# A two-layer hybrid block on one core: side transfers cut in pieces and set between weight loads, first groups paired, new layer's operand in four chains

## The chip, the cores and the metric

One core of a Trainium2 chip runs the whole program. The metric is the time of one execution in microseconds (us) on the device, from the first to the last instruction of the core and what lies around them; the smaller the better. TensorE (PE) does the matrix products, VectorE (DVE) and ScalarE (ACT) elementwise work, GpSimd (POOL) a little of it, and SyncE (SP) issues nearly all DMAs, in order.

## The reference

Two layers over a sequence of 256 tokens of width 1024, all in float32. Each layer normalizes its input, projects it to 14,352 columns, runs three branches on them (differential attention, a gated convolution of 31 taps, and a gated delta rule in chunks of 64), gates and adds what they give, and projects back onto the input.

```python
def hybrid_layer(x, cos, sin, layer_idx, norm_w, w_in, ...):
    h = rms_norm(x, norm_w)
    proj = h @ w_in
    (aq, ak, av, az, c_glu, cz, dq, dk, dvv, dz, db, da, gate_logits) = jnp.split(proj, split_points, axis=-1)
    y_a = diff_attention_branch(aq, ak, av, az, ...)
    y_c = conformer_conv_branch(c_glu, cz, ...)
    y_d = gated_deltanet_branch(dq, dk, dvv, dz, db, da, ...)
    g_a, g_c, g_d = jnp.split(jax.nn.sigmoid(gate_logits), N_BRANCHES, axis=-1)
    merged = g_a * y_a + g_c * y_c + g_d * y_d
    return x + merged @ w_out

def reference(x, positions, ...):
    cos, sin = rope_tables(positions)
    for l in range(DEPTH):
        x = hybrid_layer(x, cos, sin, l, ...)
    return rms_norm(x, final_norm_w)
```

In the convolution branch `u = a * sigmoid(g)` goes through a causal depthwise filter of 31 taps. In the delta rule the keys of each chunk make a unit lower triangular matrix, `tri`, against which a right-hand side is solved.

## The kernel before

**Weights.** All weight matrices pass through one queue of 288 chunks, 144 for each layer: 36 groups of 512 output columns, each of 4 chunks; a chunk holds two k-steps of 128 rows, [128, 2, 512], 512 KB. `load` (its DMA is L427) issues a chunk on SP into one of three buffers `w_raw`; `prepare` lets ACT round it to `w_hi`; `lows` lets DVE form the rest, `w_lo` = `w_raw` - `w_hi`. Three matmuls (hi by hi, hi by lo, lo by hi) then stand for one in float32. Once `w_lo` of chunk n is issued, `load` is called for chunk n+3, whose transfer on SP waits until the buffer has been read. `group_b` uses the activations as the stationary operand (12 matmuls per chunk), `group_a` the weights (24). Both run through `dense`, which takes one chunk after the other. I write c33 for chunk 33 of the queue.

**The planner.** The order on every engine is fixed at build time by the kernel itself. Around the dense groups, side work is written as generators ("streams"): `add` enters one with a priority, `pump` lets each issue what the planner's clock takes to be ready, `finish` and `until` wait for streams. A stream's DMA is `dma(landing, ...)`: the planner assumes that it has landed after a fixed number of us. Each engine works strictly in the order so found, so an instruction that waits longer than the planner thought holds all that stand behind it, on SP too.

**Order of a layer.** `SEQ` names the steps: v (attention values), k (delta keys), t (conv gate and value, `c_groups`), z, q, w, c (attention heads), a and others; "d1" and "d2" are convolution groups, `conv_group(1)` and `conv_group(2)`; `conv_group(3)` is called by `last_conv` in the merge of the delta branch. Channels 0 to 255 of the convolution (n = 0) are made on DVE, the rest on PE.

**Delta keys**, `dn_keys(hs, st)` (L878), once for each half hs of the heads: the diagonal 16 x 16 blocks of the triangular matrix are written to memory (`v_keep`, 64 KB) and read back spread over all partitions (`nrep`, 1 MB in two transfers; the tile is `y_hi` for hs 0 and `t` for hs 1). DVE inverts the blocks by forward substitution: `z`, 15 pairs of a product (`dn_t`) and a reduction (`dn_z`). POOL makes the block diagonal `dia` (tile `t`) from `z`, and a chain of transposes and products on PE follows.

**Convolution on PE**: `conv_load(n)` brings the taps `wd` (1 MB, one transfer) and four shifted copies of the inputs, `u` (tile `u4`, four transfers of 256 KB), which were stored to memory before (`u_keep`, 512 KB, in `evac_u`). `conv_group(n)` is 128 small matmuls.

**Start.** The input comes in transposed pieces `x_t` of 256 KB: two on ACT's queue from the first moment, then one more there and one on SP, among the first weight chunks on SP. The constants are issued on ACT before any ACT work. Only chunk 0 is loaded in two halves.

**Layer boundary.** The last group `group_out` leaves the new input of layer 2 in `big`; `raw_half` (two streams) transposes it, scales it into `h_hi` and `h_lo`, and takes its squares, before the first group "v0" may start.

Of the kernel before, what the change touches and what calls it, by code (L numbers as in the profile page):

```python
# [19 lines left out]
P = 128  # L20
# [39 lines left out]
SEQ = "v0 k0 t0 z0 k1 v1 q0 w0 c0 x0 q1 a0 d1 w1 x1 c1 z1 a1 d2".split()  # L60
# [33 lines left out]
def kernel(  # L94
# [133 lines left out]
    for k in (0, 2):  # L228
        nc.scalar.dma_start(out=xt[:, k:k + 2], in_=x_t[:, k:k + 2])
# [54 lines left out]
    class Stream:  # L284
        def __init__(self, gen, prio):
            self.gen, self.prio, self.steps, self.held, self.marks = gen, prio, [], [], False
            self.t, self.on, self.over, self.done, self.read = clk[0], "", False, False, None
# [13 lines left out]
        def serve(self, room):  # L301

            count, used = 0, 0.0
            while True:
                if not self.steps:
# [5 lines left out]
                    if self.over:  # L311
                        self.done = True
                        streams.remove(self)
                        return count + 1, used
# [9 lines left out]
                elif key in ("PE", "SP"):  # L324
# [7 lines left out]
                    else:  # L332
                        self.t = clk[0] + cost
# [22 lines left out]
    def dma(landing, **kw):  # L356
        live[0].steps.append(("SP", lambda: nc.sync.dma_start(**kw), landing))
# [59 lines left out]
    one_layer = [(ORDER.index(key), c) for key in body for c in range(NCH)]  # L417
# [5 lines left out]
    def load():  # L423
        if len(raws) < len(queue):
# [3 lines left out]
            raws.append((raw, clk[0] + 4.5))  # L428
# [13 lines left out]
    def lows(upto=-1):  # L442
        while halves and (halves[0][2] <= clk[0] + 0.3 or halves[0][0] <= upto):
# [5 lines left out]
            if kk.stop == KC:  # L449
                load()  # L450
# [44 lines left out]
    def group_b(l, key, xs, evac, need=()):  # L495
# [7 lines left out]

        return dense(l, key, step, ps, evac, need)
# [28 lines left out]
    def group_a(l, key, xs, evac, need=()):  # L533
# [15 lines left out]

        return dense(l, key, step, ps, evac, need)  # L550
# [36 lines left out]
    def raw_half(xt, l, st, q):  # L587
        yield
        xh, xl = st["h"]
        for n in range(2):  # L590
            tp = (side_tile() if n == 0 else dn_tile()).rearrange("p (j t) -> p j t", j=2)
            for j in range(2):
                k = 4 * q + 2 * n + j
                for t in range(2):
                    tr(tp[:, j, t * P:(t + 1) * P], xt[:, t, k * P:(k + 1) * P])
            for j in range(2):
                k = 4 * q + 2 * n + j
                sc = nwt[:, l * KT + k:l * KT + k + 1]
                S.activation(out=xh[:, k, :], in_=tp[:, j, :], func=AF.Copy, scale=sc)
            for j in range(2):  # L600
                k = 4 * q + 2 * n + j
                sc = nwt[:, l * KT + k:l * KT + k + 1]
# [1055 lines left out]
```

## Time and profile before

| | us |
|---|---|
| time, median of three runs | 1114.2 (1113.66, 1114.2, 1120.59) |
| time of the profiled execution | 1114.95 |
| its span, first to last instruction | 1113.2 |
| PE busy in it | 1044.5 (94%) |
| DVE busy | 866.7 (78%) |
| ACT busy | 548.3 (49%) |
| moved by DMA | 178.07 MB, mean 160 GB/s |
| mean granted clock of TensorE | 0.971 |

The profiled execution lies 0.75 us above the median and 1.75 us above its own span. "Busy" on PE counts a matmul as running also while the clock is halved, so a stretch at clock 0.5 looks busy and gets half as much done. An idle time of PE is listed with what released it, which is the last of possibly several things it waited for; what made that one late has to be followed further back, over DVE, SP and the transfers.

### The profile page before, as it was taken

How to read it: one execution, taken by the hardware profiler on the slowest of the kernel's cores; microseconds unless marked ns; L12 is line 12 of the kernel's file. 1: busy time of each engine (PE TensorE's matmuls, PEld its weight loads, DVE VectorE, ACT ScalarE, POOL GpSimd, SP SyncE). 2: the span in 40 equal slices, each digit the busy share in tenths (PEclk: the TensorE clock that was granted, in tenths of full speed). 3: DMA queues.
4: the chain of work that ended last, by engine and by line, in shares of the span. 5: the costliest groups of instructions: out<-in, count | busy, mean ns of one | idle time of the engine just before them, and what ended most of it. 6: DMA issues, size and time to landing. Idle time of an engine off the chain costs nothing.

```text
span 1113.2 us, 18028 instructions
## 1 busy us (share of the span) xinstructions
PE 1044.5 (94%) x6892; PEld 905.1 (81%) x6892; DVE 866.7 (78%) x1729; ACT 548.3 (49%) x977; POOL 102.3 (9%) x73
## 2 busy tenths in 40 slices
PE   6999759989999999999999998998989999999996
PEld 5899747889877888897889998788978777879885
DVE  4799657769766899996578979876877579989855
ACT  4564325334544556554456553534354355665543
POOL 0001001300010000121100200030000000002220
PEclk8999878989999999999999998999989999999998
DMA  6555573244535456556665566634443535645662
GB/s 215 160 163 165 177 191 114 97 135 133 159 111 148 133 172 206 169 187 193 185 206 168 153 197 213 179 114 133 135 134 110 137 117 168 212 150 174 198 207 82
DMA packets 57894, 178.07 MB, mean 160 GB/s; under 512 B 6480, under 2 KB 16336, under 8 KB 57040
## 3 DMA queue, kind: packets, MB, share of 16 engines
q1 hardware_dynamic: 56240, 175.17, 52.0%
q10 hardware_dynamic: 1568, 1.75, 0.5%
q8 instruction: 54, 0.88, 0.3%
q14 instruction: 32, 0.26, 0.1%
HBM read 172.44 MB, written 4.46 MB: 159 GB/s over the span
## 4 chain that ended last, share of the span: by engine, by line
PE 69%; DVE 17%; DMA 8%; issue 3%; ACT 2%; SPq 0%; ACTq 0%; DVEq 0%
PE acc L349 55%; PE s L347 11%; DVE w_lo L130 6%; DMA w_raw<-in_wts 4%; PE s L354 3%; DVE big L130 2%; DMA y_hi<-v_keep 1%; DMA t<-v_keep 1%; ACT w_hi L130 1%; DVE c_acc L130 1%; DVE vv L130 1%; DVE gx L130 1%; DMA big<-in_x_t 1%; DVE dn_t L130 1%; DMA u_keep<-c_u 0%
## 5 line engine op out<-in xcount | busy, mean ns | idle before, releaser
L130 ACT CAST w_hi<-w_raw 128x1024 fp32r<-128x1024 f32 (+1 forms) x289 | 302.3, 1046 | 354.7 <-PE acc L349 235.7
L130 DVE TENSOR_TENSOR w_lo<-w_raw,w_hi 128x1024 fp32r<-128x1024 f32 (+1 forms) x289 | 365.5, 1266 | 77.7 <-ACT w_hi L130 76.8
L349 PE MATMUL acc<-h_hi,w_lo 128*128 128x256 f32 x768 | 220.5, 287 | 14.3 <-DVE w_lo L130 14.1
L349 PE MATMUL acc<-h_hi,w_hi 128*128 128x256 f32 x768 | 224.5, 292 | 0.0
L349 PE MATMUL acc<-w_hi,h_hi 128*128 128x512 f32 x512 | 216.0, 422 | 6.6 <-ACT w_hi L130 6.6
L349 PE MATMUL acc<-h_lo,w_hi 128*128 128x256 f32 x768 | 219.3, 286 | 0.0
L349 PE MATMUL acc<-w_lo,h_hi 128*128 128x512 f32 x512 | 202.0, 395 | 0.6 <-DVE w_lo L130 0.6
L349 PE MATMUL acc<-w_hi,h_lo 128*128 128x512 f32 x512 | 202.2, 395 | 0.0
L349 PEld LDWEIGHTS acc<-h_hi,w_lo 128*128 128x128 f32 x768 | 149.4, 195 | 16.1 <-DVE w_lo L130 15.9
L349 PEld LDWEIGHTS acc<-h_hi,w_hi 128*128 128x128 f32 x768 | 149.7, 195 | 1.4 <-issue 1.0
L349 PEld LDWEIGHTS acc<-h_lo,w_hi 128*128 128x128 f32 x768 | 149.6, 195 | 0.3
L349 PEld LDWEIGHTS acc<-w_hi,h_hi 128*128 128x128 f32 x512 | 97.7, 191 | 26.0 <-ACT w_hi L130 6.8
L349 PEld LDWEIGHTS acc<-w_hi,h_lo 128*128 128x128 f32 x512 | 97.1, 190 | 21.7 <-DVE h_lo L130 0.2
L349 PEld LDWEIGHTS acc<-w_lo,h_hi 128*128 128x128 f32 x512 | 98.0, 191 | 17.0 <-DVE w_lo L130 1.9
L130 DVE SCALAR_TENSOR_TENSOR c_acc<-c_u,pc,c_acc 128x255 f32<-128x255 f32 (+29 forms) x120 | 51.3, 470 | 2.3 <-ACT c_acc L130 2.3
L349 PE MATMUL acc<-w_hi,y_lo 128*128 128x512 f32 x128 | 50.1, 391 | 2.0 <-DVE y_lo L130 2.0
L349 PE MATMUL acc<-w_hi,y_hi 128*128 128x512 f32 x128 | 51.5, 402 | 0.3 <-ACT y_hi L130 0.3
L349 PE MATMUL acc<-w_lo,y_hi 128*128 128x512 f32 x128 | 49.9, 390 | 0.0
L130 DVE SCALAR_TENSOR_TENSOR big<-wc,pc,big 128x255 f32<-128x255 f32 (+2 forms) x96 | 47.6, 543 | 0.5 <-ACT big L130 0.5
L349 PE MATMUL acc<-u,wd 128*32 128x256 f32 (+7 forms) x768 | 41.7, 369 | 1.8 <-ACT c_acc L130 1.8
L349 PE MATMUL acc<-w_hi,t 128*128 128x512 f32 x128 | 40.0, 389 | 0.0
L349 PEld LDWEIGHTS acc<-u,wd 128*32 128x32 f32 x768 | 23.7, 110 | 18.3 <-ACT c_acc L130 3.5
(276 smaller groups left out, 1521.1 us busy)
## 6 DMA issues: line engine op xcount, KB each, us to landing
w_raw<-in_wts SPq DMA_DIRECT2D x287, 512.0 KB, 3.8
wd<-in_cwd SPq DMA_DIRECT2D x6, 1024.0 KB
y_hi<-v_keep SPq DMA_DIRECT2D x4, 512.0 KB
u_keep<-c_u SPq DMA_DIRECT2D x4, 512.0 KB, 5.3
t<-v_keep SPq DMA_DIRECT2D x4, 512.0 KB
u<-u_keep SPq DMA_DIRECT2D x6, 256.0 KB, 6.4
u<-u_keep SPq DMA_DIRECT2D x6, 255.0 KB, 7.3
u<-u_keep SPq DMA_DIRECT2D x6, 254.0 KB, 7.2
```

What stands on the lines that cost most here:

```text
L130: step = (self.key, lambda: getattr(self.eng, op)(*args, **kw), cost)
L347: live[0].steps.append(("PE", lambda: TE.matmul(**kw), cost))
L349: TE.matmul(**kw)
L354: ("PE", lambda: TE.transpose(out=out, in_=in_, identity=ident[0:n, 0:n]), 0.11))
```

## The change

Six things are changed; no arithmetic is.

1. The planner has a model of the transfers: `dma(kb, rate)` and `transfer` keep the time at which the queue is free (0.45 us per issue) and at which the bytes have come. It replaces the fixed landing times and now also counts the weight chunks.
2. `nrep` comes in four transfers of 256 KB (`blocks`, `copies`), and `z` waits for them one by one, every fourth step. `v_keep` and the transfers that read it follow each other on SP.
3. `conv_load` brings `wd` in four transfers of 256 KB and leaves time between these and between the four of `u`.
4. In `SEQ` "d1" stands behind "x1" and not ahead of "w1"; `conv_group(3)` is called ahead of the first product of the delta branch and not ahead of its first gate group.
5. `pair` runs the first two groups of a layer (attention values, delta keys) in turn: first half of the k-steps of each, then the second half of each. The weight queue is ordered accordingly. The new layer's operand is made in four streams `raw_part`, and the squares in `raw_squares`.
6. At the start `x_t` comes on SP alone, its first piece ahead of chunk 0 and its second between the halves of chunk 0; the constants are issued on ACT behind the cast of chunk 1.

```diff
-SEQ = "v0 k0 t0 z0 k1 v1 q0 w0 c0 x0 q1 a0 d1 w1 x1 c1 z1 a1 d2".split()
+SEQ = "v0 k0 t0 z0 k1 v1 q0 w0 c0 x0 q1 a0 w1 x1 d1 c1 z1 a1 d2".split()
...
-    for k in (0, 2):
-        nc.scalar.dma_start(out=xt[:, k:k + 2], in_=x_t[:, k:k + 2])
...
-    def dma(landing, **kw):
-        live[0].steps.append(("SP", lambda: nc.sync.dma_start(**kw), landing))
+    def dma(kb, rate=280.0, **kw):
+        live[0].steps.append(("SP", lambda: nc.sync.dma_start(**kw), (kb, rate)))
+
+    def transfer(due, kb, rate=280.0):
+
+        lane[0] = max(lane[0], due, clk[0]) + 0.45
+        lane[1] = max(lane[1], lane[0] + 1.2) + kb * 1.024 / rate
+        return lane[1] + 0.6
...
-    one_layer = [(ORDER.index(key), c) for key in body for c in range(NCH)]
+    one_layer = [(ORDER.index(key), c) for half in range(2) for key in body[:2]
+                 for c in range(half * NCH // 2, (half + 1) * NCH // 2)]
+    one_layer += [(ORDER.index(key), c) for key in body[2:] for c in range(NCH)]
...
-            raws.append((raw, clk[0] + 4.5))
+                if not raws and not kk:
+                    nc.sync.dma_start(out=xt[:, 2:4], in_=x_t[:, 2:4])
+            raws.append((raw, transfer(freed, 512)))
...
+    def pair(groups, need):
+        consumed(*guards[-2:])
+        for half in range(2):
+            if half:
+                finish(*[s for n, s in need if n])
+            for l, key, step, ps, evac in groups:
+                for k in range(half * KT // 2, (half + 1) * KT // 2):
+                    if k % KC == 0:
+                        part = take((l, ORDER.index(key), k // KC))
+                    step(part, k)
+                    if k == KT - 1:
+                        guards.append(add(evac(ps), 0))
+                    if k % KC == KC - 1:
+                        spent()
+                    pump()
+        return guards[-2:]
...
+    nc.sync.dma_start(out=xt[:, 0:2], in_=x_t[:, 0:2])
     load()
-    nc.scalar.dma_start(out=xt[:, 4:6], in_=x_t[:, 4:6])
     load()
-    nc.sync.dma_start(out=xt[:, 6:8], in_=x_t[:, 6:8])
+    nc.sync.dma_start(out=xt[:, 4:8], in_=x_t[:, 4:8])
     load()
...
-            dma(3.5, out=v_keep[hs], in_=vc.rearrange("p c h i -> p (c h i)"))
-            yield 3.5
-            for half in range(2):
-                dma(0.1 if half else 7.0, out=nrep[:, 8 * half:8 * half + 8].rearrange("p j c i -> p (j c i)"),
...
-            yield 8.0
+            dma(64, out=v_keep[hs], in_=vc.rearrange("p c h i -> p (c h i)"))
+            yield 0.1
+
+            def blocks(n):
+                dma(256, 130.0, out=nrep[:, 4 * n:4 * n + 4].rearrange("p j c i -> p (j c i)"),
...
+                yield
+
+            def copies():
+                for n in range(4):
+                    s_b.append(add(blocks(n), 0.05))
+                    yield 1.8
...
+            yield from until(s_b[0])
             z = sm.tile([P, 8, 16], F32, name="dn_z", bufs=1)
             V.tensor_copy(out=z, in_=bc_mid(eye16, 8))
             for i in range(1, 16):
+                if i % 4 == 0:
+                    yield
+                    while len(s_b) <= i // 4:
+                        yield
+                    yield from until(s_b[i // 4])
...
         def conv_load(n):
-            dma(0.1, out=wd.rearrange("p f q j c -> p (f q j c)"), in_=cwd[l, n - NV])
+            for f in range(2):
+                for q in range(2):
+                    qs = slice(4 * q, 4 * q + 4)
+                    dma(256, out=wd[:, f, qs].rearrange("p q j c -> p (q j c)"),
+                        in_=cwd[l, n - NV].rearrange("p (f q x) -> p f q x", f=2, q=2)[:, f, q])
+                    yield 1.5
             while len(stored) <= n // 2:
                 yield
-            yield 3.0
+            yield from until(stored[n // 2])
             for i in range(4):
-                dma(0.1 if i < 3 else 6.0, out=u4[32 * i:32 * i + 32, :, i:T],
+                dma(256, 150.0, out=u4[32 * i:32 * i + 32, :, i:T],
                     in_=u_keep[n * 2 * P:(n + 1) * 2 * P, 0:T - i].rearrange("(g c) t -> c g t", c=32))
+                yield 2.0
...
-            if kind == "g" and not i:
+            if kind == "y" and not i:
                 conv_group(3)
```

**SP around the first delta keys and the first convolution load.** SP's order in layer 1 before, from the store of the diagonal blocks (`v_keep`) to the inputs of the first convolution group; "x4" is four transfers in a row, and 128x1x1024 is half of `nrep`.

```order
L357 DMA v_keep_85<-dn_vc 128x128
L427 DMA w_raw<-in_wts 128x1024 x4
L357 DMA y_hi<-v_keep_85 128x1x1024 x2
L427 DMA w_raw<-in_wts 128x1024 x4
L357 DMA u_keep<-c_u 128x4x256
L357 DMA wd<-in_cwd 128x2048
L357 DMA u_88<-u_keep 32x8x256
L357 DMA u_88<-u_keep 32x8x255
L357 DMA u_88<-u_keep 32x8x254
L357 DMA u_88<-u_keep 32x8x253
L427 DMA w_raw<-in_wts 128x1024 x12
```

SP's order at the same place after, up to the first two of the four `u`; the first `w_raw` here is c33.

```order
L357 DMA v_keep_85<-dn_vc 128x128
L357 DMA y_hi<-v_keep_85 128x1x512 x3
L437 DMA w_raw<-in_wts 128x1024
L357 DMA y_hi<-v_keep_85 128x1x512
L437 DMA w_raw<-in_wts 128x1024 x8
L357 DMA wd<-in_cwd 128x512
L437 DMA w_raw<-in_wts 128x1024
L357 DMA u_keep<-c_u 128x4x256
L437 DMA w_raw<-in_wts 128x1024
L357 DMA wd<-in_cwd 128x512
L437 DMA w_raw<-in_wts 128x1024
L357 DMA wd<-in_cwd 128x512
```

The four loads that stood between `v_keep` and `nrep` now stand behind three quarters of `nrep`, and no two pieces of `wd` or `u` stand side by side: each has a weight load between it and the next.

**DVE at the forward substitution of the first delta keys.** DVE's order before, from the copy that starts `z`. The `w_lo` ahead of it is that of c34, the two in it those of c35 and c36; `gt` belongs to the gate of the convolution.

```order
L130 COPY dn_z<-cst 128x128
L130 TENSOR_TENSOR dn_t_1372<-dn_z,y_hi 128x8x2
L130 TENSOR_REDUCE dn_z<-dn_t_1372 128x8
L130 TENSOR_TENSOR dn_t_1373<-dn_z,y_hi 128x8x3
L130 TENSOR_REDUCE dn_z<-dn_t_1373 128x8
L130 TENSOR_TENSOR dn_t_1374<-dn_z,y_hi 128x8x4
L130 TENSOR_REDUCE dn_z<-dn_t_1374 128x8
L130 TENSOR_TENSOR w_lo<-w_raw,w_hi 128x1024
L130 SCALAR_TENSOR_TENSOR gt<-gt,rnb 128x512 x2
L130 TENSOR_TENSOR dn_t_1388<-dn_z,y_hi 128x8x5
L130 TENSOR_TENSOR w_lo<-w_raw,w_hi 128x1024
L130 TENSOR_REDUCE dn_z<-dn_t_1388 128x8
```

After, the copy that starts `z` stands behind `w_lo` of c31. The `w_lo` in the first rows is that of c32; the rows here end with the next one, c33.

```order
L130 COPY dn_z<-cst 128x128
L130 TENSOR_TENSOR dn_t_1185<-dn_z,y_hi 128x8x2
L130 TENSOR_TENSOR w_lo<-w_raw,w_hi 128x1024
L130 TENSOR_REDUCE dn_z<-dn_t_1185 128x8
```

```order
L130 TENSOR_TENSOR dn_t_1329<-dn_z,y_hi 128x8x9
L130 TENSOR_TENSOR gt<-acc,rnb 128x512 x2
L130 TENSOR_REDUCE dn_z<-dn_t_1329 128x8
L130 TENSOR_TENSOR dn_t_1330<-dn_z,y_hi 128x8x10
L130 TENSOR_REDUCE dn_z<-dn_t_1330 128x8
L130 TENSOR_TENSOR dn_t_1362<-dn_z,y_hi 128x8x11
L130 TENSOR_REDUCE dn_z<-dn_t_1362 128x8
L130 TENSOR_TENSOR w_lo<-w_raw,w_hi 128x1024
```

Between the two pieces stand six more pairs of a product and a reduction and no `w_lo`. So the substitution starts three chunks earlier; ten reductions, nine products and two `gt` stand between `w_lo` of c32 and of c33, then four pairs ahead of `w_lo` of c34 and one product ahead of that of c35.

**SP at the start.** Before, the two first pieces of `x_t` and the third were on ACT's queue, and SP had:

```order
L427 DMA w_raw<-in_wts 128x512 x2
L427 DMA w_raw<-in_wts 128x1024
L650 DMA big<-in_x_t 128x512
L427 DMA w_raw<-in_wts 128x1024 x2
L677 DMA pc<-in_pch 128x184
```

After, all of `x_t` (tile `big`) is on SP:

```order
L680 DMA big<-in_x_t 128x512
L437 DMA w_raw<-in_wts 128x512
L439 DMA big<-in_x_t 128x512
L437 DMA w_raw<-in_wts 128x512
L437 DMA w_raw<-in_wts 128x1024
L683 DMA big<-in_x_t 128x1024
L437 DMA w_raw<-in_wts 128x1024 x2
```

What the first matmuls need now comes first and alone; the same bytes come through one queue instead of two.

More of the change, by code (lines that the diff above doesn't have):

```diff
@@ L286, in __init__ @@
             self.gen, self.prio, self.steps, self.held, self.marks = gen, prio, [], [], False
-            self.t, self.on, self.over, self.done, self.read = clk[0], "", False, False, None
+            self.t, self.on, self.over, self.done, self.read, self.land = clk[0], "", False, False, None, 0.0
         def trace(self):
@@ L332, in serve @@
                     else:
-                        self.t = clk[0] + cost
+                        self.land = max(self.land, transfer(due, *cost))
+                        self.t = lane[0]
                     self.on = key
@@ L421, with load @@
     taken = [0]
-    def load():
+    def load(freed=0.0):
         if len(raws) < len(queue):
@@ L449, in lows @@
             if kk.stop == KC:
-                load()
+                load(ready[n][2])
     halves = []
@@ L502, in step @@
                     pump()
+        if hold is not None:
+            hold.append((l, key, step, ps, evac))
+            return None
         return dense(l, key, step, ps, evac, need)
@@ L735, in norm_stream @@
             else:
-                yield from until(s_r[1][1])
+                yield from until(*s_sq)
                 st_n["rn"] = rn = inv_rms(st_n["ss"])
@@ L826 @@
         if l:
-            finish(s_r[0][1])
+            finish(*[s for q, s in s_r if not q])
         s_norm = add(norm_stream(), 0.1)
@@ L1093, in k_group @@
             s_e[hs, 0].append(group_a(l, ("in", DK + hs * GW), H, evac_dn(hs, 0, sts[hs]["kq"][:, :, 0, :]),
-                    need=raw_need()))
+                                      hold=None if hs else held))
+            if not hs:
+                s_v[0], s_e[hs, 0][0] = pair(held, raw_need())
             s_k.append(add(dn_keys(hs, sts[hs]), 0.3 + 0.1 * hs))
@@ L1119, in evac_u @@
                 yield
-                dma(3.0, out=u_keep[s * GW:(s + 1) * GW].rearrange("(a p) t -> p a t", p=P), in_=us[s])
-                stored.append(s)
+                yield from ()
+                dma(512, out=u_keep[s * GW:(s + 1) * GW].rearrange("(a p) t -> p a t", p=P), in_=us[s])
                 if s == 0 and NV:
                     taps_left[0] = conv_steps()
-                if s == 0 and NV < 2:
-                    s_cv[NV] = add(conv_load(NV))
             s_g = group_a(l, ("in", CG + s * GW), H, evac_g)
-            group_a(l, ("in", CA + s * GW), H, evac_u)
+            stored.append(group_a(l, ("in", CA + s * GW), H, evac_u))
+            if s == 0 and NV < 2:
+                s_cv[NV] = add(conv_load(NV), 0.05)
         ac = act.tile([P, 8, T], F32, name="c_acc")
@@ L1552, in f @@
                         if t:
-                            s_r.append((i, add(raw_half(xt, l + 1, st_o, i))))
+                            parts = [add(raw_part(xt, l + 1, st_o, 4 * i + 2 * n), 0) for n in range(2)]
+                            s_r.extend((i, s) for s in parts)
+                            s_sq.append(add(raw_squares(xt, st_o, i, parts), 0.1))
                         continue
```

74 lines of the change are left out of this document (41 added, 33 removed).

## The prediction

> **What bounds the kernel now.** I read the page first: which engine is full, and where it isn't.
>
> ```profile
> PE 1044.5 (94%) x6892; PEld 905.1 (81%) x6892; DVE 866.7 (78%) x1729; ACT 548.3 (49%) x977; POOL 102.3 (9%) x73
> PE   6999759989999999999999998998989999999996
> PEclk8999878989999999999999998999989999999998
> ```
>
> PE is the bound nearly everywhere. What a change of order can give is the time in which PE stands, and the time in which its clock is halved. The list of PE's waits names the first (total, times, longest):
>
> ```profile
> PE acc L349 <- DVE w_lo L130: 14.7, 6, 6.7
> PE s L354 <- POOL t L130: 11.7, 1, 11.7
> PE s L347 <- DVE y_lo L130: 8.3, 2, 4.3
> PE acc L349 <- ACT w_hi L130: 6.6, 1, 6.6
> PE s L347 <- DVE gf L130: 6.3, 2, 3.5
> PE s L347 <- DVE wc L130: 2.8, 1, 2.8
> PE acc L349 <- DVE y_lo L130: 2.0, 1, 2.0
> PE s L354 <- ACT t L130: 1.9, 1, 1.9
> ```
>
> These are 54.3 us, nearly all in a dozen places. The stretches in which the clock fell are the second; in these windows the PEclk column (the one behind POOL) stands at 0.5, and half of PE's busy time there is what the halving cost:
>
> ```profile
> 7.80:14.60 6.80, 3.31 (x7) 2.39 (x8) 4.04 (x7) 4.78 (x10) 0.00 (x0) 0.50 0.70 241
> 127.30:134.10 6.80, 2.93 (x13) 2.93 (x14) 5.20 (x14) 0.00 (x0) 0.00 (x0) 0.50 0.39 133
> 154.60:175.10 20.50, 9.51 (x30) 7.62 (x31) 13.29 (x24) 7.90 (x14) 2.41 (x2) 0.50 0.28 93
> 243.40:250.20 6.80, 5.03 (x23) 5.03 (x24) 4.20 (x11) 0.05 (x1) 0.00 (x0) 0.50 0.44 138
> 670.00:676.80 6.80, 4.66 (x22) 4.66 (x23) 6.66 (x14) 1.23 (x2) 0.00 (x0) 0.50 0.45 146
> 779.20:782.60 3.40, 3.40 (x19) 3.40 (x18) 3.30 (x10) 0.00 (x0) 0.00 (x0) 0.51 0.07 25
> 816.80:823.60 6.80, 5.40 (x25) 4.70 (x25) 4.16 (x10) 4.02 (x8) 0.00 (x0) 0.50 0.40 140
> ```
>
> PE was busy 34.2 us in them, so the halving cost 17.1. With the waits that makes 71.4 us in reach of an order.
>
> What made PE late shows in the chain that ended last (start, length). Its longest transfers are not weights only:
>
> ```profile
> 1.67 7.70 DMA big<-in_x_t
> ...
> 119.79 8.78 DMA y_hi<-v_keep
> ...
> 146.79 10.96 DMA w_raw<-in_wts
> ...
> 236.16 7.88 DMA t<-v_keep
> ...
> 660.74 7.81 DMA y_hi<-v_keep
> ...
> 770.62 7.16 DMA t<-v_keep
> ```
>
> And DVE's own waits say that it stood in front of the product that reads `nrep`, with every `w_lo` behind it:
>
> ```profile
> DVE dn_t L130 <- DMA y_hi<-v_keep: 17.0, 2, 8.7
> DVE dn_t L130 <- DMA t<-v_keep: 11.7, 2, 6.0
> ```
>
> So five of the seven largest waits (near 131, 163, 245, 672 and 779 us) are one pattern: a side transfer that was planned as landed and was not. This is what the spacing goes at.
>
> **The change part by part.** The sum is made against the profiled execution, 1114.95 us, which is 0.75 above the median.
>
> *Start.* `x_t`'s first piece shared the ring with the weights and the other pieces and took 7.70 us. PE waited 6.6 us for `w_hi`, then worked at half clock (3.31/2 = 1.65), then waited 2.8 for the squares: 11.0. Now that piece comes alone. A 512 KB weight load, twice its size, takes this long:
>
> ```profile
> w_raw<-in_wts SPq DMA_DIRECT2D x287, 512.0 KB, 3.8
> ```
>
> So about 4 us of the 7.70 go, with the half clock 1.65: 5.7, say 6. The squares' wait stays, and the bytes are the same. The four constant issues that now stand on ACT ahead of its next cast are hidden while weights still arrive; uncovered, they would delay that cast. Bounds: 3 (half of the first wait) to 8 (11.0 less the squares' wait).
>
> *First delta keys, layer 1 (near 131).* PE lost 6.7 and 2.93/2 = 1.5: 8.2. After, `z` starts three chunks earlier, and no longer waits 8.7 us. But its work now falls into a stretch where DVE is full. A substitution costs 15 pairs of these:
>
> ```profile
> L130 DVE TENSOR_REDUCE dn_z<-dn_t x60: 161/229/290, 128.9 to 810.8; 128x8 f32<-128x16 f32 x4, 128x8 f32<-128x24 f32 x4, 128x8 f32<-128x32 f32 x4, 128x8 f32<-128x40 f32 x4
> L130 DVE TENSOR_TENSOR dn_t<-dn_z,y_hi x30: 186/282/401, 128.7 to 691.6; 128x16 f32<-128x16 f32 x2, 128x24 f32<-128x24 f32 x2, 128x32 f32<-128x32 f32 x2, 128x40 f32<-128x40 f32 x2
> L130 DVE TENSOR_TENSOR w_lo<-w_raw,w_hi 128x1024 fp32r<-128x1024 f32 x6 | 7.3, 1216 | 0.0
> L130 DVE TENSOR_TENSOR gt<-acc,rnb 128x512 f32<-128x512 f32 x2 | 1.3, 678 | 0.0
> 84.00:112.00 28.00, 27.15 (x223) 26.51 (x221) 27.30 (x56) 13.26 (x20) 2.99 (x2) 1.00 0.58 170
> ```
>
> From `w_lo` of c32 to the end of `w_lo` of c33 stand 10 reductions (2.3), 9 products (2.5), 2 `gt` (1.4) and `w_lo` itself (1.2): 7.4 us. PE takes 24 matmuls for a chunk of this kind, 0.12 us apart (2.9 us):
>
> ```profile
> 33.81 0.28 PE L349 MATMUL acc<-h_hi,w_hi 128*128 128x256 f32 x1
> 33.93 0.28 PE L349 MATMUL acc<-h_lo,w_hi 128*128 128x256 f32 x1
> ```
>
> With DVE at 27.30 of 28 us before, PE has little in hand; I give it 1.5 us. 7.4 - 2.9 - 1.5 = 3.0 at c33. For c34, four pairs (2.0) and `w_lo` (1.2) against 2.9 add 0.3 to 0.9. Total 3.9, plus 0.6 for the chance of a fallen clock. It saves 8.2 - 4.5 = 3.7 (0 to 7, as PE has nothing or 4 us in hand). SP stands behind `v_keep` until that store has landed, with c33's load behind it; I take this as covered by the three raw buffers, and its price, if not, by the like wait for a stored tile, 15.7/4 = 3.9 us:
>
> ```profile
> SPq L357 <- DMA u_keep<-c_u: 15.7, 4, 4.8
> ```
>
> *First convolution load (near 163).* `wd` in one piece, the store and four `u` stood ahead of c42, whose chain piece is 10.96 us; DVE stood, POOL's `t` came late, PE lost 11.7, 2.8 (the half of the `gf` row that lies here) and 9.51/2 = 4.75: 19.2. After, a weight load stands between any two pieces, and POOL's `t` no longer has a late `w_lo` ahead of its `z`. I keep 1.2 of waiting and save 18 (bounds 12 to 19.2).
>
> *Second delta keys, layer 1 (near 245).* 4.0 and 5.03/2 = 2.5: 6.5. DVE may still stand some us before `z`, but `conv_group(1)`, moved by `SEQ`, lies there as cover for PE, 6.9 us of work without a weight chunk:
>
> ```profile
> L349 PE MATMUL acc<-u,wd 128*32 128x252 f32 (+7 forms) x128 | 6.9, 369 | 0.0
> ```
>
> Saves 6.2. If the cover is gone, DVE's wait of 6.0 comes back whole.
>
> *Layer 2.* The same four places: near 672, 6.5 + 2.3 = 8.8, of which a substitution between two `w_lo` keeps about as much as in layer 1 with clock, 5.2: saves 3.6 (0 to 8). Near 705, 1.9. Near 779, 4.3 + 1.7 = 6.0, covered. Near 818, 3.5 + 2.7 = 6.2, of which 5, since `z` is earlier. The 2.0 behind `y_lo` near 996: `conv_group(3)` now stands ahead of that product and gives DVE time; 1.0.
>
> *Pair and four chains.* At the layer boundary no wait of a size to be listed above stands, so there is nothing for them to win: 0 to 0.4. At the start the pair halves the need for `x_t` against weights; that is in the first term.
>
> *Sum.* 6 + 3.7 + 18 + 6.2 + 3.6 + 1.9 + 6.0 + 5 + 1 = 51.4. Against it I set 6 for new waits that the new order brings: the list of before shows seven of 1.9 to 4.3 us that nobody planned (18.5 in all); I take a third, bounds 0 and 18.5. 1114.95 - 51.4 + 6 = 1069.6, say **1070**.
>
> *A rule against the change.* The Trainium skill, DMA: Bandwidth & Descriptors (Measured, under Bandwidth), asks for DMAs of at least 1 MiB, and gives each DMA about 2.0 us of fixed cost; cutting `wd` and `nrep` to 256 KB goes against it. By it the 26 added transfers are an estimated 52 us of queue time. The trace shows 512 KB landing in 3.8 us while the next is already issued, so that cost overlaps as far as this case shows; it is priced from rows as the second rival.
>
> **The rivals.**
>
> *The substitution chokes `w_lo`.* It is moved into a stretch that had 0.7 us of DVE time free in 28. If PE has nothing in hand at c33 and c175, the two waits are 5 to 6 us with the clock fallen, and the third and fourth places pay 2 each: about 12 more, **1082**. For it speaks the window row above; against it, that PE can be ahead by up to three chunks.
>
> *Many small transfers.* 18 more pieces of `wd` and 8 more of `nrep`. 512 KB at the 232 GB/s of the row below is 2.2 of the 3.8 us to landing, so 1.6 are fixed. If each of the 26 holds the weights up by that, 42 us come back: **1111**, no change. For it: the ring was 79% busy in this stretch. Against: four `u` came together without a fixed part each.
>
> ```profile
> 672.00:700.00 28.00, 27.86 (x195) 26.78 (x196) 26.83 (x48) 10.13 (x12) 2.33 (x2) 0.91 0.79 232
> ```
>
> *SP's head of line, slower than before.* A `wd` or `u` piece may go only when the convolution group before has read its buffer, and it holds the weight loads behind it. The trace has this wait:
>
> ```profile
> SPq L357 <- PE acc L349: 17.1, 4, 5.2
> ```
>
> 4.3 us each. Six loads of eight pieces are 48 places. It decides from 45/48 = 0.9 us a piece that gets through to PE; at half of 4.3 it is 103 us: **1173**. Against it: a piece waits once for the group, then the other seven are free; and three raw chunks are 8 us of cover.
>
> *It doesn't do what it says.* The planner only believes its model. If `nrep` and `u` land as late as before behind the weights now set between, DVE stands as before and only the start and half of the place near 163 win: 15, so **1100**.
>
> **How the numbers follow.** Forecast (1055 to 1076) 0.52; choked `w_lo` (1076 to 1090) 0.22; small transfers (1090 to 1115) 0.10; not as it says (1090 to 1104) 0.06; SP's head of line, slower, 0.03; better than forecast, with the two substitutions free and no new wait (1114.95 - 51.4 - 8.1 = 1055 and below), 0.07. A measurement of this kernel can tell about 1% (11 us) from no change: faster is under 1103. Of the small transfers 0.05 and of not as it says 0.01 lie above that, so faster 0.91, same 0.06, slower 0.03. The range leaves out the last fifth: 1052 to 1092. It takes in the bounds of the two substitutions (7.3 and 8 us) and of the new waits, though not all at once.
>
> A word on the clock allowance: the wait of 2.8 us (`wc`) brought no halving by itself, the one of 3.5 (`gf`) did. The Trainium skill, TensorE: Matmul & The Clock Gate (Part 1: The HAM clock gate), has the clock fall after an idle window of about 3.4 us; the two rows agree. By that rule the 3.0 us at c33 and its copy would cost no clock, the 0.6 and 1.3 set for it would go, and the sum would be 1067.7.
>
> **What would show it.** Right: first matmul near 7 us; DVE's waits for `y_hi<-v_keep` and `t<-v_keep` together below 10 us where they were 28.7; no wait of PE for POOL's `t` above 2; no half clock from 154 to 175; a wait for `w_lo` of 2 to 5 us near 115 to 125 and its copy in layer 2. Wrong: a `w_lo` wait above 6 there; weight loads that take over 6 us while `wd` and `u` pass; PE waiting for `c_acc` or `u` ahead of the moved convolution group; more than 20 us of waits in places where before had none.

## The result and the profile after

The changed kernel takes 1077.3 us, median of four runs (1075.49 to 1080.76), beside 1113.93 for the kernel before in the same comparison: a ratio of 0.9667 (95% interval 0.9617 to 0.9718). The profiled execution took 1075.49 us, 39.5 less than the one before; the sum of the prediction, made against that one, said 45.4 less. Of the prediction's bands the median lies at the lower edge of the one for the choked `w_lo` (1076 to 1090), the profiled execution in the forecast (1055 to 1076).

From the page: busy times, and the slices of PE and of its clock.

```profile
PE 1036.9 (97%) x6892; PEld 897.6 (84%) x6892; DVE 875.2 (82%) x1729; ACT 546.9 (51%) x977; POOL 105.3 (10%) x73
PE   8999799999999999999999979999999999999896
PEclk9999999999999999999999989999999999999998
```

The matmuls are the same; PE's busy time fell by 7.6 us, and less of it lies under a halved clock (below). The rest of the 39.5 us is idle time. PE's waits (total, times, longest):

```profile
PE acc L349 <- ACT w_hi L130: 11.0, 3, 5.5
PE acc L349 <- DVE w_lo L130: 3.5, 4, 1.2
PE acc L349 <- ACT t L130: 2.9, 1, 2.9
PE s L347 <- DVE gf L130: 1.2, 1, 1.2
PE s L347 <- DVE gx L130: 1.1, 2, 0.9
```

The waits for POOL's `t` (11.7), for `y_lo` (8.3) and for `w_lo` (14.7) have gone or shrunk. One row has grown, from 6.6 to 11.0: PE waits for the cast of a weight chunk. DVE's waits in front of the substitution fell from 28.7 to 14.4 us, not below the 10 that the prediction named as a sign:

```profile
DVE dn_t L130 <- DMA y_hi<-v_keep: 7.5, 4, 2.9
DVE dn_t L130 <- DMA t<-v_keep: 6.9, 2, 4.2
```

Two of the three waits for the cast sit at c33 and at the like place in layer 2, c175 (the third, 1.55 us, is the start). PE in the timeline, with the wait before each matmul in brackets (the last row is in layer 2):

```profile
117.44 0.39 PE L349 MATMUL acc<-h_hi,w_hi 128*128 128x256 f32 x1 [4.02 <-ACT w_hi L130]
118.70 0.58 PE L349 MATMUL acc<-h_hi,w_lo 128*128 128x256 f32 x1 [0.76 <-DVE w_lo L130]
638.85 0.58 PE L349 MATMUL acc<-h_hi,w_hi 128*128 128x256 f32 x1 [5.45 <-ACT w_hi L130]
```

Why the cast is late stands in SP's timeline and in the chain of waits, whose pieces there are the store and c33's load:

```profile
100.23 0.33 SPq L437 DMA_DIRECT2D w_raw<-in_wts  x1
100.59 0.43 SPq L357 DMA_DIRECT2D v_keep<-dn_vc  x1
104.60 2.36 SPq L357 DMA_DIRECT2D y_hi<-v_keep  x3
107.07 0.38 SPq L437 DMA_DIRECT2D w_raw<-in_wts  x1
107.50 0.60 SPq L357 DMA_DIRECT2D y_hi<-v_keep  x1
```

```profile
100.59 3.99 DMA v_keep<-dn_vc
107.07 9.18 DMA w_raw<-in_wts
```

SP stood 3.6 us behind the store, then issued three blocks of `nrep`; c33's load went out at 107.07 and needed 9.18 us, where the median load needs 3.8. Two windows of the transfers (the last two columns are the busy share of the DMA engines and GB/s) show the blocks of `nrep` alone, at about half the rate, and then together with the weights:

```profile
106.00:110.00 4.00, 3.86 (x33) 3.65 (x31) 1.06 (x4) 0.00 (x0) 0.00 (x0) 1.00 0.44 137
110.00:116.00 6.00, 2.90 (x22) 2.69 (x22) 4.68 (x18) 0.00 (x0) 0.00 (x0) 1.00 1.03 264
```

The stretches in which the clock stood at 0.5 (column ahead of those two):

```profile
118.70:122.10 3.40, 3.40 (x16) 3.40 (x17) 3.16 (x9) 2.76 (x3) 0.00 (x0) 0.51 0.56 172
637.50:644.30 6.80, 4.24 (x18) 3.95 (x19) 6.42 (x16) 3.14 (x3) 0.00 (x0) 0.50 0.53 168
1006.00:1009.40 3.40, 3.40 (x10) 2.71 (x9) 1.29 (x3) 0.32 (x1) 0.00 (x0) 0.52 0.38 131
```

There were seven before. Half of PE's busy time here, 5.5 us, is what they cost (17.1 before). The column misses one: PE's first matmuls, from 6.39 to 12.4 us, are 0.43 us apart or more, and those of the same form behind them 0.23, while the column stands at 1.00. That start costs another 3.0 us by estimate (half of 6.0), more than the 1.65 of before.

What ended just before PE could go on at c33, on DVE and ACT (the first row is `w_lo` of c30, which frees the buffer of c33; the second the last reduction ahead of `w_lo` of c33):

```profile
101.71 1.22 DVE L130 TENSOR_TENSOR w_lo<-w_raw,w_hi 128x1024 fp32r<-128x1024 f32 x1
117.08 0.25 DVE L130 TENSOR_REDUCE dn_z<-dn_t 128x8 f32<-128x88 f32 x1
116.35 1.04 ACT L130 CAST w_hi<-w_raw 128x1024 fp32r<-128x1024 f32 x1 [10.81 <-DMA w_raw<-in_wts]
```

The substitution ended at 117.33 and the cast at 117.39: two causes held PE to the same moment. Between the two `w_lo` of c31 and c33 DVE had itself stood 2.94 and 0.91 us for blocks of `nrep`.

### The profile page after: what moved, and what is told of

Same layout as the page of the kernel before. It is cut to its first block, busy times and chain, and to the rows that moved or that the text cites. A ratio compares the mean times of both kernels' runs of the same rounds, so it can differ in the third digit from the quotient of the medians.

```text
span 1073.7 us, 18066 instructions
## 1 busy us (share of the span) xinstructions
PE 1036.9 (97%) x6892; PEld 897.6 (84%) x6892; DVE 875.2 (82%) x1729; ACT 546.9 (51%) x977; POOL 105.3 (10%) x73
## 4 chain that ended last, share of the span: by engine, by line
PE 78%; DVE 14%; DMA 3%; issue 2%; ACT 2%; SPq 0%; ACTq 0%; DVEq 0%
PE acc L349 64%; PE s L347 11%; DVE w_lo L130 5%; PE s L354 3%; DMA w_raw<-in_wts 2%; DVE big L130 1%; DVE wa L130 1%; DVE c_acc L130 1%; DVE gx L130 1%; ACT w_hi L130 1%; DVE dn_vc L130 1%; DMA y_hi<-v_keep 1%; DVE tz L130 0%; DVE y_lo L130 0%; DMA v_keep<-dn_vc 0%
## 5 line engine op out<-in xcount | busy, mean ns | idle before, releaser
L130 DVE TENSOR_TENSOR w_lo<-w_raw,w_hi 128x1024 fp32r<-128x1024 f32 (+1 forms) x289 | 369.7, 1280 | 69.9 <-ACT w_hi L130 68.4
L349 PEld LDWEIGHTS acc<-w_hi,h_lo 128*128 128x128 f32 x512 | 96.8, 189 | 21.3
L130 DVE SCALAR_TENSOR_TENSOR big<-wc,pc,big 128x255 f32<-128x255 f32 (+2 forms) x96 | 50.6, 568 | 0.0
L130 POOL TENSOR_TENSOR wa<-wa 128x512 f32<-128x512 f32 x16 | 22.6, 1409 | 195.5 <-DVE wa L130 127.0
```

The source lines that it names most:

```text
L130: step = (self.key, lambda: getattr(self.eng, op)(*args, **kw), cost)
L349: TE.matmul(**kw)
```

## The experiments

All runs stand beside the kernel before on their chip; each has four or five timed executions.

| run | us, median (range) | ratio to before, 95% interval |
|---|---|---|
| control | 1076.43 (1072.56 to 1077.07) | 0.9618 (0.957 to 0.9665) |
| one_load | 1074.55 (1071.6 to 1077.56) | 0.9608 (0.9559 to 0.9657) |
| block_then_load | 1079.35 (1077.98 to 1080.32) | 0.965 (0.9605 to 0.9696) |
| conv3_early | 1086.5 (1085.71 to 1087.54) | 0.9713 (0.9659 to 0.9767) |
| start_old | 1079.82 (1078.05 to 1082.93) | 0.9664 (0.9627 to 0.9701) |
| no_pair | 1078.15 (1076.85 to 1080.4) | 0.9653 (0.9613 to 0.9693) |
| conv_together | 1069.38 (1067.19 to 1072.31) | 0.9569 (0.9533 to 0.9606) |
| d1_early | 1077.48 (1075.45 to 1079.11) | 0.9639 (0.9604 to 0.9675) |
| conv_bunched | 1078.74 (1075.89 to 1080.83) | 0.9673 (0.9637 to 0.9709) |
| nrep_quarter | 1073.01 (1070.97 to 1073.82) | 0.9621 (0.9588 to 0.9653) |
| pool_queue | 1070.51 (1069.39 to 1071.24) | 0.9603 (0.9566 to 0.964) |
| pool_lane | 1070.56 (1068.98 to 1072.08) | 0.9594 (0.9559 to 0.9628) |

A caution holds for all: the planner decides anew behind every edit, so the order of the later stages changes too. What a run says of a place is read at that place; its total holds the replanned rest as well. The runs were made in four groups on different chips, on which the kernel before took 1118.6 us (control to conv3_early), 1118.9 (start_old to d1_early), 1115.4 (conv_bunched to pool_queue) and 1118.1 (pool_lane); across groups the ratios compare better than the medians.

### The changed kernel again

> The changed kernel once more, beside the others on one chip. All theories: 1075 to 1081 us, PE's idle time about 26 us, with the two waits for the cast of c33 and c175 (4.0 and 5.5 us) in the same places.

The waits for the cast are 4.09 and 6.98 us here (5.45 in the second place of the first profile), so the second varies by 1.5 us from one execution to another.

### What is late at c33: the order on SP

```diff
             dma(64, out=v_keep[hs], in_=vc.rearrange("p c h i -> p (c h i)"))
             yield 0.1
+            loads = len(raws)
+            while len(raws) < loads + 1:
+                yield
```

> One weight load (c33's in layer 1) goes between the store of v_keep and the reads of nrep, so SP's wait for the store no longer holds it and none of nrep is ahead of it. Theory Q (the load was late because it stood behind the store's wait and three blocks): the waits near 117 and 639 for the cast, 5.4 and 6.7 us with what follows, and their half clock go; 1065 to 1070. Theory R (nrep's 1 MB shares the transfers with the weights, wherever it stands): the wait moves to the next chunk and stays at 3 to 5 us; 1074 to 1078. Theory D (the substitution chokes w_lo): now 11 pairs stand between w_lo of c32 and of c33, so PE waits 2 to 4 us for w_lo in place of the cast; 1071 to 1076.

c33's load went out at 102.74, ahead of `nrep`, and came in time. The wait moved to c34, whose load now shared the transfers with `nrep`: 3.43 us at 118.59, and 3.04 and 0.98 in layer 2. That is theory R's place and size; the time, 1.9 us below the control, is not clear of noise.

```diff
                     s_b.append(add(blocks(n), 0.05))
-                    yield 1.8
+                    loads = len(raws)
+                    while len(raws) < loads + 1:
+                        yield
```

> Each block of nrep goes once another weight load has gone: store, block, load, block, load, block, load, block. SP still waits for the store with c33's load behind it, but only 256 KB instead of 768 KB are ahead of that load, and three or four pairs of the substitution stand between two w_lo instead of ten. Theory Q, if SP's wait of 4 us alone makes the load late: the cast of c33 still comes 2 us late or more, 1072 to 1077. Theory R, if the blocks ahead of it do: the load lands in 5 to 6 us instead of 9.2 and PE waits less than 1 us; 1065 to 1070. Theory D: no wait of PE for w_lo above 1 us here.

None was right alone. PE's waits in layer 1 became 1.77, 0.85 and 0.95 us, each for `w_lo`, together 3.6 at c33 to c36, so the loss was spread and not removed. But no wait for the cast of c33 was left, though its load still stood behind the store: with one block ahead of it in place of three, SP's stand alone was covered. In layer 2 a wait of 2.66 us for the cast stayed. Three kernels with different orders on SP (control 4.9, one_load 3.9, block_then_load 3.6) lose about as much at this place: there is more than one cause.

### The bytes of nrep, and SP's queue

```diff
-                dma(256, 130.0, out=nrep[:, 4 * n:4 * n + 4].rearrange("p j c i -> p (j c i)"),
-                    in_=v_keep[hs].rearrange("(b h j) n -> h b (j n)", b=8, h=4)[n].unsqueeze(1).to_broadcast(
-                        [8, 16, 4 * P]))
+                dma(256, 130.0, out=nrep[:, 4 * n:4 * n + 1].rearrange("p j c i -> p (j c i)"),
+                    in_=v_keep[hs].rearrange("(b h j) n -> h b (j n)", b=8, h=4)[n][:, 0:P].unsqueeze(1).to_broadcast(
+                        [8, 16, P]))
```

> Leaves out three quarters of nrep's bytes: each of the four transfers brings 64 KB instead of 256 KB, the rest of the tile is zeros set early on POOL; the order on the engines is that of the changed kernel. Theory R (nrep's bytes are slow and the weights queue behind them): c33's load lands in 5 us or less after issue and PE's wait for the cast near 117 and 639 falls from 4.1 and 7.0 to below 1.5; 1064 to 1070. Theory D (the substitution's DVE work is the limit once the load is there): PE waits 2.5 to 4 us for w_lo instead; 1071 to 1075. Theory H (SP's wait for the store): 2 to 4 us of the wait for the cast stay; 1071 to 1076.

c33's load landed in 5.9 us instead of 8.9 (control), and the wait for its cast fell from 4.09 to 1.17. But PE then waited 2.08 us for the `w_lo` of the same chunk; in layer 2 it was 1.61 and 3.65. PE's two rows, where the control has 3.6 and 12.8:

```profile
PE acc L349 <- DVE w_lo L130: 8.4, 6, 3.6
PE acc L349 <- ACT w_hi L130: 4.5, 5, 1.6
```

So R holds for the load, and behind it stands D, the cause that the prediction had named; the time is in D's range, and the ratio, 0.9621, is the control's.

```diff
-    def dma(kb, rate=280.0, **kw):
-        live[0].steps.append(("SP", lambda: nc.sync.dma_start(**kw), (kb, rate)))
+    def dma(kb, rate=280.0, queue=None, **kw):
+        live[0].steps.append(("SP", lambda: (queue or nc.sync).dma_start(**kw), (kb, rate)))
...
-            dma(64, out=v_keep[hs], in_=vc.rearrange("p c h i -> p (c h i)"))
+            dma(64, queue=nc.gpsimd, out=v_keep[hs], in_=vc.rearrange("p c h i -> p (c h i)"))
...
-                dma(256, 130.0, out=nrep[:, 4 * n:4 * n + 4].rearrange("p j c i -> p (j c i)"),
+                dma(256, 130.0, queue=nc.gpsimd, out=nrep[:, 4 * n:4 * n + 4].rearrange("p j c i -> p (j c i)"),
```

(on the kernel of conv_together, below)

> The run with wd in one piece and u together, and besides the store of v_keep and nrep's four blocks are issued by POOL instead of SP, so that the weights neither wait for the store nor queue behind the blocks on SP. Theories R and H together: PE's waits for the cast near 117 and 639 go, 5 and 8 us with clock, but DVE's substitution costs 2 to 3 us there; 1060 to 1065 beside the 1069 of its base. If transfers issued by POOL come later or slower than SP's by 3 us or more, z and the chain behind it are late and a wait for POOL's t takes its place: 1068 to 1075.

Here the swap is clean. In the timeline, the cast of c33 came at 110.48, six us earlier than in the changed kernel, and PE still waited 4.01 us at the same time as before, now for DVE (5.25 us in layer 2):

```profile
110.48 1.05 ACT L130 CAST w_hi<-w_raw 128x1024 fp32r<-128x1024 f32 x1 [1.10 <-DMA w_raw<-in_wts]
117.84 0.41 PE L349 MATMUL acc<-h_hi,w_lo 128*128 128x256 f32 x1 [4.01 <-DVE w_lo L130]
```

The total did not fall below the base's 1069.4: it lies in the range of the second case, without that case's wait for POOL's `t`. The loads of c31 to c33 took 8.4 to 9.0 us here, with no block ahead of them on SP: `nrep`'s bytes slow the weights from another queue too.

```diff
+    lane, pool_lane = [0.0, 0.0], [0.0, 0.0]
...
-        live[0].steps.append(("SP", lambda: (queue or nc.sync).dma_start(**kw), (kb, rate)))
+        live[0].steps.append(("SP", lambda: (queue or nc.sync).dma_start(**kw),
+                              (kb, rate, pool_lane if queue else lane)))
```

(on the kernel of pool_queue; `transfer` then keeps the times of the two queues apart)

> As the run with POOL's queue, and besides the planner keeps a second transfer model for that queue, so it no longer thinks the weights late and puts two or three pairs of the substitution between two w_lo where ten stood ahead of c33's. The two causes that hold the places near 117 and 639, the late load and the ten pairs ahead of w_lo, are taken away together, where each run before took one. If these two are all: the waits of PE there, 4.8 and 5.3 us in the base with 6 us of half clock, fall below 2 us each and no half clock stands there; 1060 to 1066. If DVE lacks the time in that stretch however it is ordered (16.7 us of its work for 14.4 us of PE's): waits of 3 to 5 us for w_lo in all, spread over several chunks; 1066 to 1071.

At the place the first case came out: DVE makes a `w_lo` every 2.3 to 3.1 us, and PE's longest waits are 0.76 us in layer 1 and 0.68, 0.65 and 0.79 in layer 2, with no half clock. DVE's `w_lo` of c33 to c36 in the timeline:

```profile
112.09 1.22 DVE L130 TENSOR_TENSOR w_lo<-w_raw,w_hi 128x1024 fp32r<-128x1024 f32 x1
114.56 1.22 DVE L130 TENSOR_TENSOR w_lo<-w_raw,w_hi 128x1024 fp32r<-128x1024 f32 x1
117.38 1.22 DVE L130 TENSOR_TENSOR w_lo<-w_raw,w_hi 128x1024 fp32r<-128x1024 f32 x1
119.68 1.22 DVE L130 TENSOR_TENSOR w_lo<-w_raw,w_hi 128x1024 fp32r<-128x1024 f32 x1
```

But the total stayed at 1070.6. PE reached c38 at 127.8 (134.8 in pool_queue) and c178 at 640.0 (649.1), seven and nine us ahead, and c280 only 0.5 ahead. Part of what was given back stands in waits for `dn_r`, the delta chain's own results, behind the second keys of each layer:

```profile
262.71 0.49 PE L347 MATMUL s<-big,a_at 128*128 128x128 f32 x2 [2.68 <-DVE dn_r L130]
785.28 0.94 PE L347 MATMUL s<-big,a_at 128*128 128x128 f32 x6 [3.69 <-DVE dn_r L130]
```

Each is followed by half clock; the one in layer 1 stood in pool_queue too (2.38), the one in layer 2 is new. The rest I did not settle: side work that PE did earlier in one kernel than in the other also moves such a distance without being a loss.

### What removed the wait near 163

```diff
-            for f in range(2):
-                for q in range(2):
-                    qs = slice(4 * q, 4 * q + 4)
-                    dma(256, out=wd[:, f, qs].rearrange("p q j c -> p (q j c)"),
-                        in_=cwd[l, n - NV].rearrange("p (f q x) -> p f q x", f=2, q=2)[:, f, q])
-                    yield 1.5
+            dma(1024, out=wd.rearrange("p f q j c -> p (f q j c)"), in_=cwd[l, n - NV])
...
-                yield 2.0
```

> wd comes in one transfer of 1 MB and the four u side by side again, where the new planner puts them; the rest as changed. By the prediction the spacing is worth most of 18 us at the first convolution load: 1086 to 1095, with PE waiting 8 us or more for POOL's t or a cast near 145 to 175. Rival: it was not the pieces but the model of the transfers (the planner now counts the weights behind them and waits for nrep in blocks) that took the wait away: 1074 to 1081, no such wait above 3 us.

The rival was right about the wait, and the time is below both ranges: the lowest median of all, some 7 us below the control and 8 below d1_early on the same chip. PE has no wait of 0.3 us or more between 119 and 166, and 1.25 us there. (In the changed kernel the four `u` of this place go out at 154.0, 156.3, 161.3 and 165.5, with a weight load between any two.) PE's rows:

```profile
PE acc L349 <- ACT w_hi L130: 10.6, 3, 5.0
PE acc L349 <- DVE w_lo L130: 6.9, 7, 1.8
PE s L347 <- DVE dn_r L130: 2.7, 2, 2.4
```

The 7 us do not come from this place: PE is level with the control at c96 (395.4 and 395.8). They come from three later ones, near 430 (waits of 0.91 and 0.81 gone), near 640 (the cast's wait 5.02 instead of 6.98) and near 1007 (`t`, 3.04, gone). The second of these varies from one execution to another. That they went because of the pieces, and not by the new plan alone, is not shown.

In the next run the four `u` follow the store and `wd` at once, SP's order of before at this place:

```diff
+            if n == NV:
+                while not sent:
+                    yield
+            dma(1024, out=wd.rearrange("p f q j c -> p (f q j c)"), in_=cwd[l, n - NV])
-            while len(stored) <= n // 2:
+            while len(sent) <= n // 2:
                 yield
-            yield from until(stored[n // 2])
+            yield 0.1
...
                 dma(512, out=u_keep[s * GW:(s + 1) * GW].rearrange("(a p) t -> p a t", p=P), in_=us[s])
+                yield
+                sent.append(s)
```

> As the run with wd in one piece, but the four u also follow the store of u and wd at once, with no weight load between: SP's order at this place is that of before. The rest as changed, z early included. Theory B (the bunch on SP, store, wait for it to land, 2 MB, then weights, made the 11.7 and 2.8 us near 163): 8 to 19 us of waits come back there, 1080 to 1090. Theory Z (the substitution being three to eight chunks earlier did it; the bunch only mattered because z stood behind the w_lo it held up): waits there below 4 us, 1068 to 1076.

At the place theory Z holds. SP stands 5.4 us behind the store, with c43's load behind four `u`:

```profile
138.94 0.43 SPq L357 DMA_DIRECT2D u_keep<-c_u  x1
139.42 0.50 SPq L357 DMA_DIRECT2D wd<-in_cwd  x1
145.27 1.81 SPq L357 DMA_DIRECT2D u<-u_keep  x4
147.18 0.40 SPq L437 DMA_DIRECT2D w_raw<-in_wts  x1
```

and PE waits 1.16 us at 149.7 and nothing above 0.4 from there to 192. c43's cast could start only at 156.11, and its `w_lo` was done 0.25 us before PE needed it: the bunch was covered here, though narrowly. PE is level with conv_together at c96 (395.8 and 395.4). The time, 9 us above conv_together, is in the range given for theory B, but not for its reason: the half clock stands in five stretches (near 8, 25, 122, 640 and 867), and a wait of 2.6 for `o_d` lies near 865. Whether the bunched loads of layer 2 brought that was not tried.

### The start, the pair, and the places of the convolution groups

> The start goes back: the pieces of x_t on two queues as before and the constants issued early; the rest, pair included, as changed. By the prediction's first term the new start is worth 6 us (3 to 8), so 1080 to 1084 beside 1076 to 1077 of the changed kernel; the first matmul of a weight chunk at 10 to 11 us with half clock behind it. Rival: the pair alone makes the start (the first four chunks need only half of x_t), then the old transfers cost 2 us or less: 1077 to 1079.

The transfers and constants of the start as before, the rest as changed. The first wait is back:

```profile
PE acc L351 <- ACT w_hi L130: 17.2, 3, 6.4
```

The 6.4 is the start's. PE's first matmul comes at 11.27 where the control has 6.04, but on c32 only 1.8 us are left (112.07 and 110.28): the control waits 0.55 and 1.56 us at 20 and 22 and then runs at half clock for 3.4, and this run does not. (The half clock behind its first matmul came as well: the matmuls are 0.43 us apart or more until 17 us.) The medians differ by 3.4. Neither is clear of noise: kernels with the new start and the pair reach c32 anywhere from 108.7 to 112.0. So the transfers of the start alone are not shown to be worth 6 us.

```diff
-            s_v.append(group_b(l, ("in", AV + i * GW), H, evac_v(i), hold=None if i else held))
+            s_v.append(group_b(l, ("in", AV + i * GW), H, evac_v(i), need=raw_need()))
...
-                                      hold=None if hs else held))
-            if not hs:
-                s_v[0], s_e[hs, 0][0] = pair(held, raw_need())
+                                      need=raw_need()))
```

(with the queue of chunks in its old order)

> The first two groups run one after the other as before; start, four chains and the rest as changed. The prediction gave the pair 0 to 0.4 us at the layer boundary: 1076 to 1079, with a wait for h_lo or h_hi below 1 us at the boundary, and at the start a wait for the second half of x_t of 1 to 3 us. Rival: the pair is what hides the start's transfers and the boundary's chains: 1081 to 1085.

As forecast: 1.7 us more, within the ranges, and not clear of noise. At the start a wait of 2.17 us for `h_hi` appears, PE's first matmul on c32 comes 1.48 us later (111.76 and 110.28, within the spread just named), and no wait above 0.4 us stands at the layer boundary. If the pair is worth something, it is at the start.

```diff
-SEQ = "v0 k0 t0 z0 k1 v1 q0 w0 c0 x0 q1 a0 w1 x1 d1 c1 z1 a1 d2".split()
+SEQ = "v0 k0 t0 z0 k1 v1 q0 w0 c0 x0 q1 a0 d1 w1 x1 c1 z1 a1 d2".split()
```

> Convolution group 1 goes back ahead of w1 in the order of steps; the rest as changed. By the prediction that group is what covers DVE's wait for t<-v_keep at the second delta keys (6.2 and 6.0 us in the two layers): if so PE waits 3 to 6 us there in each layer and the time is 1081 to 1089. Rival: z's earlier transfers by themselves hide it, the place of the group is worth nothing: 1075 to 1079.

The rival: 1077.48, and PE's waits at the second keys are 0.56 and 0.92 us. The earlier substitution hides its transfers without that cover.

```diff
-            if kind == "y" and not i:
+            if kind == "g" and not i:
                 conv_group(3)
```

> The third convolution group goes back ahead of the first gate group of the delta branch; the rest is as changed. If the new wait of 2.9 us near 1005 (PE for ACT's t of the convolution branch, with 1.6 us of half clock behind it) comes from that group's later place, it goes and the 2.0 us behind y_lo come back, 1073 to 1077. If it comes from elsewhere, it stays and the time is 1077 to 1081.

Neither case. The wait near 1005 did go, so it does come with the group's later place; but others came where the delta branch begins its first product, and the kernel is 10 us slower than the control:

```profile
PE s L354 <- DVE o_d L130: 9.2, 3, 4.9
PE s L354 <- DVE a_pe L130: 4.2, 2, 2.9
```

With the rest as changed, the place given to this group is worth some 10 us, where the prediction gave it 1.0. That it is seven us of PE work without a weight chunk, in front of a chain on DVE, is the likely reason.

## Why the prediction was right, and where not

The time lies within the range, 7 us above the point. By the steps of the changed kernel, saved as forecast and as measured from the two profiles (waits and half clock together):

| step | forecast | measured | how |
|---|---|---|---|
| start | 6 | 6.0 | PE's first matmul on c32, 115.44 and 109.46 |
| first keys | 3.7 | 1.1 | 8.2 less 4.02 + 0.76 + 0.67 (w_lo, at 110.5) + 3.40/2 |
| near 163 | 18 | 18.0 | 1.2 left |
| second keys | 6.2 | 6.5 | no wait left |
| copy near 672 | 3.6 | 0 | 8.8 less 5.45 + 1.21 + 4.24/2 |
| 705, 779, 818, 996 | 13.9 | 14.9 | waits of 0.31 and 0.89 left |
| new waits | -6 | -6.3 | 2.90 + 3.40/2 near 1005, 0.91 and 0.81 near 428 |

**The step that failed** is the one that took c33's load behind SP's stand as covered by the three raw buffers and put the bytes of `nrep` ahead of it at nothing. The two places still cost 15.9 us where 9.7 were forecast, and this 6.2 is nearly the whole distance of 5.9 between the sum and the profile. The trace gives the cover. c33's buffer was free at 102.9 and PE ready for the chunk at 113.4; with the median 3.8 us and the cast of 1.05 that leaves 5.5 us in hand. SP's stand and the issue of three blocks held the load for 4.1 us, and behind the blocks it took 9.18, 5.4 more than the median. Each alone was covered, the two together were not: 4.1 + 5.4 - 5.5 = 4.0, and PE waited 4.02. With a quarter of the bytes (nrep_quarter) the same sum is 3.7 + 2.0 - 4.6 = 1.1, and PE waited 1.17; in layer 2 of the changed kernel it is 5.6 + 4.7 - 4.9 = 5.4 for 5.45 (there the late issue alone is 0.7 more than the cover).

**The substitution's price was right in size, and stood behind the late load.** 3.0 us at c33 and 3.9 in all were forecast for `w_lo`; with the load out of the way it measured 2.08 (nrep_quarter) and 4.01 (pool_queue). The 1.5 us that PE was given in hand were 0.8 to 1.0 (`w_lo` of c28 to c31). Both causes ended at nearly the same time, so taking one away brought little; pool_lane, which takes away both, has 0.8 us of wait in layer 1 at c32 and nothing at c33.

**Three terms were right by luck.** The 18 us were put to the spacing of the pieces; conv_together and conv_bunched show that the bunched transfers cost PE nothing at that place once `z` is done before them. In the kernel before, the 11.7 was POOL waiting for a substitution that stood behind a late `w_lo` (DVE waited 9.59 us for its cast). That the earlier substitution removed it is what is left, and not shown directly: no run puts `z` back late, or takes the planner's model of the transfers away, with the rest as changed. The cover by `conv_group(1)` was not needed either (d1_early). And the 6 us of the start are made up otherwise than forecast: the first matmul came 4.9 us earlier, the half clock behind it did not go (3.0 by estimate, 1.65 before), and the wait for the squares, said to stay, fell from 2.77 to 0.65.

**A slip in the sum.** The waits of 1.9 to 4.3 us in the list of before that were called seven and 18.5 us are 21.3 us in all, and 18.5 is six of them; a third would have been 7.1 in place of 6. The 6.3 us measured for new waits is near the allowance, but none of the places was foreseen.

**The rivals.** The choked `w_lo` is real, at 4.0 and 5.3 us (pool_queue), and hidden by the load. Small transfers were no burden of the size feared: `wd` whole is some 7 us faster, but not where the pieces of the first load pass. SP's head of line, the slower case, did not come: its wait for convolution work fell from 17.1 to 5.3 us, in five waits. That the change does not do what it says did not come, though DVE still stood 14.4 us for `nrep`.

## What to carry to other kernels

When a wait is taken away, look for the second cause that ends at about the same time: it costs nothing in the profile until the first is gone, and an experiment on one alone shows no gain. The cover that buffers give is a number to be read from the trace, from the moment a buffer is free to the moment its chunk is needed, less load and cast: here 5.5 us, enough for a late issue or a slow transfer, not for both. And a term can come out right for a wrong reason, so undo the parts one by one before keeping them: here the spacing of the pieces was not what brought the gain, and the kernel without it had the lowest time, 1069.4 us.

## What the hardware showed that was not expected

**Halved clock after short waits.** The prediction read from before that 2.8 us of waiting brings no halving. Control and nrep_quarter have the same waits at the start, 0.5 and 1.56 us, two us apart:

```profile
22.30 0.50 PE L349 MATMUL acc<-w_lo,h_hi 128*128 128x512 f32 x1 [1.56 <-DVE w_lo L130]
```

```profile
22.34 0.50 PE L349 MATMUL acc<-w_lo,h_hi 128*128 128x512 f32 x1 [1.56 <-DVE w_lo L130]
```

Behind them the granted clock was 0.50 in the control and 1.00 in nrep_quarter, and PE ran 8 matmuls in the one and 13 in the other:

```profile
23.00:25.70 2.70, 2.70 (x8) 2.07 (x7) 2.63 (x6) 1.76 (x4) 0.00 (x0) 0.50 0.63 194
```

```profile
23.00:25.70 2.70, 2.70 (x13) 1.99 (x11) 2.63 (x6) 1.80 (x4) 0.00 (x0) 1.00 0.68 194
```

The wait for `t` near 1005 shows the same: after 2.90 us in the changed kernel the clock fell, after 3.04 in the control it stayed at 1.00. So a wait of 1.5 to 3 us may cost its own length or some 1.5 to 3 more. The Trainium skill, TensorE: Matmul & The Clock Gate (Part 1: The HAM clock gate), calls the window free-running, which fits that like waits end differently; but it has the clock fall after an idle window of about 3.4 us, and here 2.1 us of waiting within three were enough. The measurement decides.

**A half clock that the column does not hold.** At the start of the changed kernel the clock column is 1.00, and yet the matmuls there are 0.43 us apart until 12.4 us and 0.23 from then on. The starts of the matmuls are the surer sign.

**Slow reads of `nrep`.** While its blocks passed alone (106 to 110 us), the DMA engines were busy 0.44 of the time, which is 7 of 16, at 137 GB/s; with weights behind them it was 1.03 and 264. The single packets were not slow: one of 2 KB took 84 ns, one of 4 KB of the weights 159. So the blocks ran on fewer engines at a time. Each block reads its stored rows sixteen times, in an access pattern whose outer dimension is 8. Whether that is the reason was not tried.
